# Inverse square roots: from a seed and three Newton steps on VectorE to one power instruction on GpSimd

## The chip, the cores and the metric

The kernel runs on one core of a Trainium2 chip, in one launch. The metric is device microseconds. TensorE (PE) multiplies matrices into PSUM, VectorE (DVE) and ScalarE (ACT) work on tiles in SBUF and PSUM, GpSimd (POOL) works on tiles in SBUF and issues some DMAs, SyncE (SP) issues most DMAs. Each engine takes its instructions in the order of its own program, and waits at an instruction whose operands aren't there.

## The reference

Two blocks of a network on 512 tokens of 1024 channels, in float32: in the first a pooling mixer, attention and two gated feed-forward layers; in the second, twice, a layer that mixes four branches (a sparse attention, a retention, a recurrence of the RWKV kind, a short convolution), then cross attention to a memory of 256 tokens, then a feed-forward layer. Norms stand before and after the parts. Three computations in it need an inverse square root:

```python
def rmsnorm(x, g):
    y = xf * lax.rsqrt(jnp.mean(xf * xf, axis=-1, keepdims=True) + EPS)
def head_norm(u, eps):
    return (u - mu) * lax.rsqrt(var + eps)
```

and the unit length of the keys in the recurrence, per head and token.

## The kernel before

Activations are kept with channels on the 128 partitions: eight tiles of 128 x 512 for 1024 channels. To multiply in float32, weights and activations are split into a high part (hi) and the rest (lo); each 128 x 128 weight chunk is fetched by SP (tile wraw), its high part made by ScalarE (whi, L346) and the rest by VectorE (wlo, L347, 128 x 1024), and three matmuls (L356 to L358) follow for each input tile. A matmul of 512 columns is the common unit on TensorE.

A norm works in steps. As the tiles of x are made, ScalarE squares them (L422), GpSimd adds the squares up (L431, tile sq), and TensorE sums them over the channels with tokens on the partitions (L449, `stat_sum`): one number per token, 128 x 4 for all 512 tokens or 128 x 2 for a half. `stat_end` then takes mean and epsilon on VectorE (L463, tile rstv), calls `rsqrt`, spreads the result over all partitions by four transposes on TensorE (L467) and copies it to SBUF on ScalarE (L468, tile rstd). For a norm before a part, the part's first matmuls are started on the unscaled x ("lead", tiles hhi and hlo), and the factor is applied when their results leave PSUM; the statistic so runs beside matmuls. For a norm after a part (`post`), the normed tiles need the factor: VectorE multiplies (L932, or L929 in the final norm of the first block) and adds to x (L935), then splits into hhi and hlo (L395). In four of these (`post` with fill) products for the memory's keys and values (`mem_kv`, tile vm, L874 and L876) run on TensorE meanwhile. The last norm of the kernel goes by halves of the tokens, with half of the additions on GpSimd, and ends in the output's DMAs.

`head_norm` (eight calls: four in the recurrence, whose result is transposed at L1266, four in the retention, transposed at L1492) takes the variance at L1008 (tile hn, 128 x 8), calls `rsqrt` and multiplies at L1010. The keys' unit length (four calls) is limited at L1076 (tile kn, 128 x 8), goes through `rsqrt`, is spread by a copy (L1079) and transposed (L1082). Macc is the sum of the four branches, which GpSimd adds up at L1536.

`rsqrt` itself (L397 to L408) shifts the number's bits right by one (L402), subtracts them from a constant (L403), halves and negates the number (L404), and takes three Newton steps of three operations each (L406 to L408), all on VectorE, on tiles of 2, 4 or 8 columns; tile rs is its scratch. There are 33 calls: 21 from `stat_end`, 8 from `head_norm`, 4 for keys.

The program is written as one sequence of such calls. A scheduler then orders each engine's instructions by its own estimates of when they will be ready, so an instruction that is shorter, longer or on another engine moves others too.

Of the kernel before, what the change touches and what calls it, by code (L numbers as in the profile page):

```python
# [10 lines left out]
F32 = mybir.dt.float32  # L11
F32R = mybir.dt.float32r
I32 = mybir.dt.int32
AF = mybir.ActivationFunctionType
OP = mybir.AluOpType
AX = mybir.AxisListType

P = 128
# [21 lines left out]
# ---------------------------------------------------------------- host layout  # L40
# [112 lines left out]
def pack(inputs):  # L153
# [24 lines left out]
    # second block  # L178
# [49 lines left out]
# ---------------------------------------------------------------- kernel  # L228
class Two:
    """Eight column tiles kept in two tiles of four."""  # L230
# [8 lines left out]
class Kern:  # L239
    def __init__(self, ctx, tc, a, vat):  # L240
        self.tc, self.nc, self.a, self.vat = tc, tc.nc, a, vat
        pool = lambda name, bufs, **k: ctx.enter_context(tc.tile_pool(name=name, bufs=bufs, **k))
        self.const = pool("const", 1)
        self.big = pool("big", 1)
        self.wp = pool("wp", 3)
        self.wk = pool("wk", 2)
        self.ps = pool("ps", 1, space=bass.MemoryType.PSUM)
        self.turn, self.dtags, self.led, self.held = 0, ("pmm", "pr"), [], []
        self.dram = pool("dram", 2, space=bass.MemoryType.DRAM)
        nc = self.nc  # L250
        self.x = self.bigt("x", F32, "rbig")
        self.cst = self.const.tile([P, _CONST.n], F32, name="cst")
        self.vec = self.const.tile([P, a["vec"].shape[1]], F32, name="vec")
        nv = vat["norm_mix0"][1]
        nc.scalar.dma_start(self.vec[:, :nv], a["vec"][:, :nv])
        one = self.const.tile([P, 1], F32, name="one")
        nc.vector.memset(one, 0.0)
        nc.scalar.activation(one, one, AF.Exp)
        first = self.leads("pool_in")
        raws = self.half("w01", F32).rearrange("p k t -> p (k t)").rearrange("p (c k m) -> p c k m", c=2, k=KD)  # L260
        raws = [raws[:, 0], raws[:, 1], self.wtile("wraw")]
        self.held = [(self.wtile("whi"), self.wtile("wlo")) for _ in range(3)]

        def xload(ks):
            for k in ks:
                nc.sync.dma_start(self.x[:, k], a["xT"][:, k])

        xload([0])
        for part, then in ((slice(0, 4), (1, 2, 3)), (slice(4, 8), (4, 5, 6, 7))):
            for raw, ap, (hi, lo) in zip(raws, first, self.held):  # L270
                nc.sync.dma_start(raw[:, part], ap[:, part])
                nc.scalar.activation(hi[:, part], raw[:, part], AF.Copy)  # L272
                nc.vector.tensor_sub(lo[:, part], raw[:, part], hi[:, part])
            xload(then)
        nc.sync.dma_start(self.cst, a["cst"])
        nc.sync.dma_start(self.vec[:, nv:], a["vec"][:, nv:])
        self.load_phase(_CONST1, a["cst1"])
        self.ident = self.c("ident")
        self.ones = self.c("ones")[:, 0:1]
        self.nsplit = 0  # L280

    # ---- small pieces
# [67 lines left out]
    def products(self, ps, wt, xh, xl, ks, cols, first=True, last=True):  # L350
        """ps[:, cols] (+)= the chunk wt's products with x's tiles ks, in three exact-split passes."""
        nc = self.nc
        hi, lo = wt
        for i, k in ks:
            a, z = first and i == ks[0][0], last and i == ks[-1][0]
            nc.tensor.matmul(ps[:, cols], hi[:, i], xh[:, k, cols], start=a, stop=False)  # L356
            nc.tensor.matmul(ps[:, cols], hi[:, i], xl[:, k, cols], start=False, stop=False)  # L357
            nc.tensor.matmul(ps[:, cols], lo[:, i], xh[:, k, cols], start=False, stop=z)  # L358

    def hold(self, aps):  # L360
        """Fetches the chunks that the next lead starts with."""
        self.held = [self.weights(ap) for ap in aps]

    def dense(self, ap, xh, xl, ks=None, width=T, ps=None, then=()):
        """ps[128 cols, width] = W^T x for the column chunk ap [128, kt, 128]; the chunks then are fetched behind it."""
# [9 lines left out]
    def lead(self, aps, xh, xl, nh, order=range(KD)):  # L375
        """Starts the chunks aps together, following x's tiles as they come; the next calls of dense return them."""
# [20 lines left out]
    def rsqrt(self, out, v, n):  # L397
        """out = v ** -0.5 on [128, n], v positive and normal."""
        nc = self.nc
        s = self.wk.tile([P, 3, 16], F32, name="rs", tag="rs", bufs=2)  # L400
        i, h, t = s[:, 0, :n], s[:, 1, :n], s[:, 2, :n]
        nc.vector.tensor_scalar(i.bitcast(I32), v.bitcast(I32), 1, None, op0=OP.logical_shift_right)  # L402
        nc.vector.tensor_scalar(out.bitcast(I32), i.bitcast(I32), -1.0, float(0x5F3759DF), op0=OP.mult, op1=OP.add)  # L403
        nc.vector.tensor_scalar(h, v, -0.5, None, op0=OP.mult)  # L404
        for _ in range(3):
            nc.vector.tensor_mul(t, out, out)  # L406
            nc.vector.tensor_mul(t, t, h)  # L407
            nc.vector.scalar_tensor_tensor(out, t, 1.5, out, op0=OP.add, op1=OP.mult)  # L408

    # ---- rms norm of a feature-major tile: statistics  # L410
# [5 lines left out]
    def stat_feed(self, st, src, last, half=None, lazy=False):  # L416
        """Adds the squares of src, all of a tile or one half of its tokens, to the statistics."""
# [23 lines left out]
    def stat_sum(self, st, hs):  # L441
        """The sums over the channels, tokens on partitions."""
# [9 lines left out]
    def stat_end(self, st, half=None):  # L452
        """rstd, the same on all partitions, of the tokens of one half or of both."""
# [20 lines left out]
    # ---- pre-norm: x * g split, statistics running along  # L474
# [19 lines left out]
    # ================================================================ first block  # L494
    def leads(self, what, i=0):
        """The chunks that a part starts with."""
# [39 lines left out]
    def proj_add(self, w, hi, lo, nxt, then):  # L536
        """x += w^T (hi + lo), feeding the next norm."""
# [7 lines left out]
    def ffn(self, i, pn, nxt_name):  # L545
        """With nxt_name, feeds the next norm; without, ends in the final norm and feeds the second block's first."""
# [49 lines left out]
    def rope(self, pa, pb, c, s, dst, j):  # L596
        """Rotates halves pa/pb (4 heads) into dst[:, j:j+2], two heads to a tile, halves interleaved."""
# [15 lines left out]
    def pipelined(items, first, second, depth=1):  # L613
        """second(item) comes depth items after first(item)."""
# [10 lines left out]
    def cls(ap, g, b):  # L625
        """Columns (tokens) of block b of group g, of a [.., T] access pattern."""
# [5 lines left out]
    def natural(ap, g):  # L632
        """[.., (block, position)] viewed in token order."""
# [5 lines left out]
    def tok(ap, g):  # L639
        """[.., T] split to match natural()."""  # L640
# [4 lines left out]
    def attention(self, pn, nxt):  # L645
# [30 lines left out]
        # scores, softmax, values  # L676
# [47 lines left out]
        for g in range(3):  # L724
            hs = slice(H0[g], H0[g] + HG[g])
            st = self.wk.tile([P, 4, 2], F32, name=f"st{g}", bufs=1)
            # group statistics: -max and sum over heads of den * exp(m - max)
# [67 lines left out]
    # ================================================================ second block  # L795
    def bias_tables(self):
        """Relative bias by distance, queries on partitions: [:, h, c] for distance q - c + 384."""
# [47 lines left out]
    def mem_kv(self, i, count, hl, psums):  # L845
        """The next count chunks of the memory's keys [P, 8, 256], feature-major, and values [P, 2, 1024], to DRAM.

        hl is a place for the split memory. Returns what emits the products, which hang on nothing else."""
# [54 lines left out]
    def post(self, w, xh, xl, y, add, gname, nxt, then=(), out=None, fill=None):  # L903
        """y (+)= W^T x over the column chunks w, then x += rmsnorm(y) * g (x = rmsnorm(x) * g where y is x).

        The last chunks go by halves of the tokens, so that the norm of one half runs beside the other's products."""
# [14 lines left out]
        def norm(group):  # L921
            """The normed tiles of the (tile, columns, half) in group, one stage behind another."""
# [52 lines left out]
    # ---- mixers  # L975
# [13 lines left out]
    def sigmoid(self, out, src, bias=0.0):  # L989
        """sigmoid(src + 2 * bias) through tanh."""  # L990
# [3 lines left out]
    def head_norm(self, alloc, y, nseg, eps):  # L994
        """(y - mean) * rstd over the last 64 of PSUM y [P, nseg, 64], to SBUF."""
# [17 lines left out]
    def rwkv_in(self, l):  # L1013
        """Token-shifted projections: r, k, v (two tiles each) and the low-rank inputs."""
# [20 lines left out]
    def rwkv(self, l, j, out):  # L1035
        """Heads 2j and 2j + 1, in chunks of 64 tokens; out [P, T] feature-major."""
# [12 lines left out]
        # decay  # L1049
# [14 lines left out]
        # a, gate  # L1064
# [4 lines left out]
        # normalised k  # L1069
# [19 lines left out]
        # scaled operands  # L1089
# [12 lines left out]
        # bonus: sum over channels of r k r_k, times v  # L1102
# [6 lines left out]
        # token-major copies  # L1109
# [11 lines left out]
        # products within a chunk  # L1121
# [11 lines left out]
        # inverse of I - A: blocks of 16 by substitution, then doubled twice  # L1133
# [78 lines left out]
        # the chunks in order  # L1212
# [61 lines left out]
    def nsa(self, l, W, out, cw):  # L1274
# [9 lines left out]
        # selected and window keys and values  # L1284
# [5 lines left out]
        # gates, token-major: [P, 4, 12]  # L1290
# [28 lines left out]
        # compressed keys and values  # L1319
# [109 lines left out]
    def retention_in(self, l, W, vN):  # L1429
        """Rotated q, k in W[:, 0:4], token-major v in the two tiles vN."""  # L1430
# [17 lines left out]
    def retention_gate(self, on, hi, lo):  # L1448
        """Splits silu(g) * on."""
# [9 lines left out]
    def retention(self, l, W, vN):  # L1459
        """Normalised heads times half the gain, feature-major, in place of vN."""  # L1460
# [55 lines left out]
    def merge(self, m, hi, lo, acc, out=None, ns=range(KD)):  # L1516
        """acc (+)= 2 sigmoid(gate m) * branch m; the last one splits half of the sum into out."""
# [195 lines left out]
```

## Time and profile before

| | |
|---|---|
| median of 3 runs | 3460.29 us (3453.46 to 3465.56) |
| span of the profiled execution, first to last instruction | 3453.0 us, the only time of its own that it has |
| mean granted TensorE clock | 0.983 |
| TensorE (PE) busy | 97% |
| VectorE (DVE) busy | 53% |
| ScalarE (ACT) busy | 34% |
| GpSimd (POOL) busy | 11% |

The span lies 7.3 us under the median of the runs and inside their range. In a timeline the first two columns are the start and the duration in us, then engine, line and operation, the tiles written and read, their shapes, the count of instructions merged into the row, and in brackets the idle time before it and what ended it. A matmul of 512 columns is shown with 0.39 us, but matmuls overlap: the next one starts 0.22 to 0.23 us after it.

### The profile page before, as it was taken

Reading aid. Unit: us, or ns where it says so; the run is one execution under the profiler, and the core shown is the slowest. Engines: PE = TensorE matmul, PEld = TensorE weight load, DVE = VectorE, ACT = ScalarE, POOL = GpSimd, SP = SyncE. Lnnn points to the kernel's source line nnn. Section 1 sums busy time; section 2 is a strip of 40 time slices with the busy share of each in tenths; the row PEclk is TensorE's granted clock in tenths of the full one; section 3 lists DMA queues with packets and bytes.
Section 4 is the critical chain, followed back from the end, with each engine's and each line's share of the span. In section 5 each row is a group of like instructions: output and inputs, shape, how many; then the busy total and the mean of one; then the engine's idle time right before and its main releaser. Section 6 shows DMA issues by size and latency. Waiting matters only on the chain. (4 is left out here: it accounts for less than half of the span.)

```text
span 3453.0 us, 41910 instructions
## 1 busy us (share of the span) xinstructions
PE 3358.4 (97%) x16382; PEld 2685.1 (78%) x16382; DVE 1829.7 (53%) x3340; ACT 1168.0 (34%) x1947; POOL 391.5 (11%) x328
## 2 busy tenths in 40 slices
PE   8999999999999999999999999998999999999997
PEld 6888888787888777777887788886777788688886
DVE  7554444445544465656455544556565644664445
ACT  4332232443322323322244433342332234343332
POOL 3200012001000120101220200012010122120001
PEclk9999999989999999999999999999999999999998
DMA  3323235223222330232242333333123223223332
GB/s 131 104 98 96 93 103 155 77 86 115 95 97 94 102 105 32 72 106 87 93 145 68 104 98 98 98 110 115 34 56 96 88 92 124 84 68 98 98 98 67
DMA packets 105718, 326.29 MB, mean 94 GB/s; under 512 B 13288, under 2 KB 16880, under 8 KB 103472
## 3 DMA queue, kind: packets, MB, share of 16 engines
q1 hardware_dynamic: 99600, 295.68, 26.3%
q10 hardware_dynamic: 3232, 19.28, 1.5%
q0 software_dynamic: 2688, 8.66, 1.2%
q8 instruction: 128, 2.10, 0.3%
q14 instruction: 70, 0.57, 0.1%
HBM read 305.47 MB, written 11.81 MB: 92 GB/s over the span
## 5 line engine op out<-in xcount | busy, mean ns | idle before, releaser
L346 ACT ACTIVATE whi<-wraw 128x1024 fp32r<-128x1024 f32 (+3 forms) x593 | 565.0, 954 | 1605.8 <-PE pmm L357 638.9
L347 DVE TENSOR_TENSOR wlo<-wraw,whi 128x1024 fp32r<-128x1024 f32 (+3 forms) x593 | 654.3, 1104 | 217.4 <-ACT whi L346 212.5
L357 PE MATMUL pmm<-hlo,whi 128*128 128x512 f32 (+1 forms) x1504 | 599.2, 398 | 13.1 <-DVE hlo L395 12.8
L358 PE MATMUL pmm<-hhi,wlo 128*128 128x512 f32 (+1 forms) x1504 | 597.7, 397 | 1.7 <-DVE wlo L347 1.7
L356 PE MATMUL pmm<-hhi,whi 128*128 128x512 f32 (+1 forms) x1504 | 597.5, 397 | 0.0
L357 PE MATMUL pr<-hlo,whi 128*128 128x512 f32 (+1 forms) x1048 | 411.2, 392 | 10.2 <-DVE hlo L395 9.8
L356 PE MATMUL pr<-hhi,whi 128*128 128x512 f32 (+1 forms) x1048 | 409.8, 391 | 9.3 <-ACT whi L272 6.4
L358 PE MATMUL pr<-hhi,wlo 128*128 128x512 f32 (+1 forms) x1048 | 409.1, 391 | 0.8 <-DVE wlo L347 0.8
L431 POOL TENSOR_TENSOR sq<-sq 128x512 f32<-128x512 f32 (+1 forms) x130 | 181.2, 1394 | 1784.3 <-ACT sq L422 1754.2
L357 PEld LDWEIGHTS pmm<-hlo,whi 128*128 128x128 f32 x1504 | 285.9, 190 | 83.5 <-DVE hlo L395 18.4
L358 PEld LDWEIGHTS pmm<-hhi,wlo 128*128 128x128 f32 x1504 | 286.1, 190 | 64.4 <-DVE wlo L347 4.6
L356 PEld LDWEIGHTS pmm<-hhi,whi 128*128 128x128 f32 x1504 | 285.5, 190 | 58.8 <-issue 1.0
L357 PEld LDWEIGHTS pr<-hlo,whi 128*128 128x128 f32 x1048 | 199.6, 190 | 55.4 <-DVE hlo L395 15.5
L356 PEld LDWEIGHTS pr<-hhi,whi 128*128 128x128 f32 x1048 | 199.5, 190 | 51.1 <-ACT whi L272 6.3
L358 PEld LDWEIGHTS pr<-hhi,wlo 128*128 128x128 f32 x1048 | 199.4, 190 | 44.1 <-DVE wlo L347 4.0
L1536 POOL TENSOR_TENSOR macc<-macc,g 128x512 f32<-128x512 f32 x48 | 69.6, 1452 | 347.9 <-DVE g L1535 240.0
L358 PE MATMUL pmm<-ahi,wlo 128*128 128x512 f32 x240 | 93.4, 389 | 0.0
L356 PE MATMUL pr<-ahi,whi 128*128 128x512 f32 x240 | 93.4, 389 | 0.0
L357 PE MATMUL pr<-alo,whi 128*128 128x512 f32 x240 | 93.4, 389 | 0.0
L358 PE MATMUL pr<-ahi,wlo 128*128 128x512 f32 x240 | 93.4, 389 | 0.0
L356 PE MATMUL pmm<-ahi,whi 128*128 128x512 f32 x240 | 93.4, 389 | 0.0
L357 PE MATMUL pmm<-alo,whi 128*128 128x512 f32 x240 | 93.4, 389 | 0.0
(517 smaller groups left out, 5413.5 us busy)
## 6 DMA issues: line engine op xcount, KB each, us to landing
wraw<-w_in SPq DMA_DIRECT2D x116, 512.0 KB, 3.3
wraw<-mlp SPq DMA_DIRECT2D x64, 512.0 KB, 3.2
wraw<-mlp SPq DMA_DIRECT2D x128, 256.0 KB, 2.8
wraw<-ffn_g SPq DMA_DIRECT2D x44, 512.0 KB, 3.2
wraw<-ffn_u SPq DMA_DIRECT2D x44, 512.0 KB, 3.2
wraw<-wkv SPq DMA_DIRECT2D x32, 512.0 KB, 3.3
wraw<-ffn_d SPq DMA_DIRECT2D x32, 448.0 KB, 3.4
wraw<-qkv SPq DMA_DIRECT2D x24, 512.0 KB, 3.5
```

Of the source, the lines that this page charges most:

```text
L346: nc.scalar.activation(hi[:, :kt, :m], raw[:, :kt, :m], AF.Copy)
L347: nc.vector.tensor_sub(lo[:, :kt, :m], raw[:, :kt, :m], hi[:, :kt, :m])
L356: nc.tensor.matmul(ps[:, cols], hi[:, i], xh[:, k, cols], start=a, stop=False)
L357: nc.tensor.matmul(ps[:, cols], hi[:, i], xl[:, k, cols], start=False, stop=False)
L358: nc.tensor.matmul(ps[:, cols], lo[:, i], xh[:, k, cols], start=False, stop=z)
L431: nc.gpsimd.tensor_add(sq[:, c], acc[h][:, c], sq[:, c])
L1536: nc.gpsimd.tensor_add(acc[:, n], acc[:, n], g)
```

## The change

`rsqrt` becomes one instruction on GpSimd that raises the tile to the power -0.5, with a tile of eight columns of -0.5 that is filled once at the start. Comments and docstrings go too, so line numbers shift by 2 ahead of `rsqrt` and by 6 behind it.

```diff
         nc.scalar.activation(one, one, AF.Exp)
+        self.neghalf = self.const.tile([P, 8], F32, name="neghalf")
+        nc.vector.memset(self.neghalf, -0.5)
...
     def rsqrt(self, out, v, n):
         nc = self.nc
-        s = self.wk.tile([P, 3, 16], F32, name="rs", tag="rs", bufs=2)
-        i, h, t = s[:, 0, :n], s[:, 1, :n], s[:, 2, :n]
-        nc.vector.tensor_scalar(i.bitcast(I32), v.bitcast(I32), 1, None, op0=OP.logical_shift_right)
-        nc.vector.tensor_scalar(out.bitcast(I32), i.bitcast(I32), -1.0, float(0x5F3759DF), op0=OP.mult, op1=OP.add)
-        nc.vector.tensor_scalar(h, v, -0.5, None, op0=OP.mult)
-        for _ in range(3):
-            nc.vector.tensor_mul(t, out, out)
-            nc.vector.tensor_mul(t, t, h)
-            nc.vector.scalar_tensor_tensor(out, t, 1.5, out, op0=OP.add, op1=OP.mult)
+        nc.gpsimd.tensor_tensor(out, v, self.neghalf[:, :n], op=OP.pow)
```

VectorE has 396 instructions fewer and one memset more, GpSimd 33 more. The scheduler moves rows on all engines. VectorE at the norm before the first cross attention (its first results leave PSUM at L1583, after the change L1577), before:

```order
L347 TENSOR_TENSOR wlo<-wraw,whi 128x1024 x2
L463 TENSOR_SCALAR rstv<-pax 128x4
L347 TENSOR_TENSOR wlo<-wraw,whi 128x1024
L402 TENSOR_SCALAR rs<-rstv 128x4
L404 TENSOR_SCALAR rs<-rstv 128x4
L403 TENSOR_SCALAR rstv<-rs 128x4
L406 TENSOR_TENSOR rs<-rstv 128x4
L407 TENSOR_TENSOR rs<-rs 128x4
L408 SCALAR_TENSOR_TENSOR rstv<-rs,rstv 128x4
```

and after, where L457 is the old L463 and L349 the old L347:

```order
L397 SCALAR_TENSOR_TENSOR hlo<-x,vec,hhi 128x512 x3
L349 TENSOR_TENSOR wlo<-wraw,whi 128x1024 x2
L457 TENSOR_SCALAR rstv<-pax 128x4
L349 TENSOR_TENSOR wlo<-wraw,whi 128x1024
L1577 SCALAR_TENSOR_TENSOR xq<-pmm,rstd 128x512
```

L406 to L408 come twice more in the first before L1583 follows; in the second a weight split still stands right behind the statistic. TensorE at the same norm before, from the sums (L449) on; 17 matmuls stand between them and the transposes, of which the last six are shown:

```order
L356 MATMUL pr<-hhi,whi 128x512
L357 MATMUL pr<-hlo,whi 128x512
L358 MATMUL pr<-hhi,wlo 128x512
L356 MATMUL pr<-hhi,whi 128x512
L357 MATMUL pr<-hlo,whi 128x512
L467 MATMUL pax<-cst,rstv 128x128 x4
```

and after, where L443 are the sums and L461 the transposes:

```order
L443 MATMUL pax<-cst,sq 128x1 x4
L358 MATMUL pr<-hhi,whi 128x512
L359 MATMUL pr<-hlo,whi 128x512
L360 MATMUL pr<-hhi,wlo 128x512
L358 MATMUL pr<-hhi,whi 128x512
L359 MATMUL pr<-hlo,whi 128x512
L461 MATMUL pax<-cst,rstv 128x128 x4
```

Twelve matmuls have moved from ahead of the transposes to behind them. Elsewhere the counts between the last sum or product and the transposes go, before to after: 17 to 5 at four norms, 21 to 4 and 24 to 2 at two more, 30 to 4 at three of the four norms with fill products and 33 to 7 at the fourth, 17 to 4 and 20 to 6 at the keys, 44 to 28 and 64 to 42 at the recurrence's head norms, 34, 35, 34 and 33 to 19, 22, 19 and 19 at the retention's; in the stretch of halves 51 to 13, 73 to 4 and 19 to 4; at two norms 60 stay, at three none.

GpSimd at the end of the first layer's recurrence, before (L1269 adds the recurrence's bonus, L1536 the branches):

```order
L602 TENSOR_TENSOR ra<-ra,rt 128x512
L606 TENSOR_TENSOR rb<-rb,rt 128x512
L1536 TENSOR_TENSOR macc<-macc,g 128x512 x2
L1269 TENSOR_TENSOR yt<-yt,rz 128x512
L1536 TENSOR_TENSOR macc<-macc,g 128x512 x6
```

and after (L402 is the power, L1263 and L1530 the two additions):

```order
L596 TENSOR_TENSOR ra<-ra,rt 128x512
L600 TENSOR_TENSOR rb<-rb,rt 128x512
L402 TENSOR_TENSOR hn<-hn,neghalf 128x8
L1263 TENSOR_TENSOR yt<-yt,rz 128x512
L1530 TENSOR_TENSOR macc<-macc,g 128x512 x4
L402 TENSOR_TENSOR hn<-hn,neghalf 128x8 x2
L1530 TENSOR_TENSOR macc<-macc,g 128x512 x4
```

The recurrence's last power and the addition that hangs on it have moved ahead of the branches' additions; the retention's two powers stand between those.

## Rows read from the trace of the kernel before

**Rows 1.** The page's first part: busy us, share of the span, instructions

```profile
PE 3358.4 (97%) x16382; PEld 2685.1 (78%) x16382; DVE 1829.7 (53%) x3340; ACT 1168.0 (34%) x1947; POOL 391.5 (11%) x328
```

**Rows 2.** Waits: engine, line, what ended them, us, times, longest

```profile
PE pax L467 <- DVE rstv L408: 12.5, 5, 6.6
```

**Rows 3.** Tile rs: operation, count, ns shortest/median/longest, first and last start

```profile
L407 DVE TENSOR_TENSOR rs<-rs x99: 148/163/1283, 31.8 to 3437.8; 128x4 f32<-128x4 f32 x42, 128x8 f32<-128x8 f32 x36, 128x2 f32<-128x2 f32 x21
```

**Rows 4.** Timelines of two uncovered statistics: start us, duration, engine, line, [idle before]

```profile
1193.88 0.16 DVE L463 TENSOR_SCALAR rstv<-pax 128x4 f32<-128x4 f32 x1 [1.09 <-PE pax L449]
...
1196.37 1.09 PE L467 MATMUL pax<-cst,rstv 128*128 128x128 f32 x4 [2.52 <-DVE rstv L408]
...
2346.93 0.65 PE L467 MATMUL pax<-cst,rstv 128*128 128x128 f32 x4 [2.43 <-DVE rstv L408]
```

**Rows 5.** Timeline of one covered statistic (DVE, then PE)

```profile
1829.04 0.16 DVE L463 TENSOR_SCALAR rstv<-pax 128x4 f32<-128x4 f32 x1
1829.12 1.22 DVE L347 TENSOR_TENSOR wlo<-wraw,whi 128x1024 fp32r<-128x1024 f32 x1
...
1832.62 0.39 PE L357 MATMUL pr<-hlo,whi 128*128 128x512 f32 x1
1832.84 0.60 PE L467 MATMUL pax<-cst,rstv 128*128 128x128 f32 x4
```

**Rows 6.** Timeline of one normalised k (DVE, then PE)

```profile
1252.87 0.17 DVE L1076 TENSOR_SCALAR kn<-pr 128x8 f32<-128x8 f32 x1 [1.19 <-PE pr L1074]
...
1256.30 0.43 DVE L1079 COPY kb<-kn 128x512 f32<-128x512 f32 x1
...
1256.78 0.66 PE L1082 MATMUL pr<-cst,kb 128*128 128x128 f32 x4
```

**Rows 7.** Who waited for tile hn (us, times)

```profile
  PE pr L1266: 2.4, 2
```

**Rows 8.** Stretches: length, PE, PEld, DVE, ACT, POOL busy, PEclk, DMA share, GB/s

```profile
1796.70:1818.00 21.30, 16.83 (x84) 13.10 (x82) 21.30 (x26) 11.29 (x17) 11.39 (x8) 0.92 0.58 209
...
3056.00:3100.00 44.00, 39.56 (x258) 35.70 (x258) 39.86 (x106) 21.23 (x48) 14.13 (x16) 0.92 0.19 62
...
35.00:80.00 45.00, 37.19 (x153) 28.93 (x151) 42.55 (x87) 16.52 (x29) 16.45 (x12) 0.92 0.17 56
```

**Rows 9.** Timeline of VectorE at one statistic with fill products behind it

```profile
1791.68 0.16 DVE L463 TENSOR_SCALAR rstv<-pax 128x4 f32<-128x4 f32 x1 [1.53 <-PE pax L449]
...
1793.82 1.22 DVE L347 TENSOR_TENSOR wlo<-wraw,whi 128x1024 fp32r<-128x1024 f32 x1
...
1795.15 0.16 DVE L408 SCALAR_TENSOR_TENSOR rstv<-rs,rstv 128x4 f32<-128x4 f32 x1
1796.36 0.42 DVE L874 TENSOR_TENSOR vm<-pr,mr 128x256 f32<-128x256 f32 x1 [1.05 <-PE pr L358]
1796.71 1.41 DVE L932 SCALAR_TENSOR_TENSOR pt<-yb,vec,rstd 128x512 f32<-128x512 f32 x2
```

**Rows 10.** Timeline of the last statistic (DVE, then PE)

```profile
3432.23 0.16 DVE L463 TENSOR_SCALAR rstv<-pax 128x2 f32<-128x2 f32 x1 [0.64 <-PE pax L449]
...
3438.53 0.16 DVE L408 SCALAR_TENSOR_TENSOR rstv<-rs,rstv 128x2 f32<-128x2 f32 x1
...
3438.84 0.66 PE L467 MATMUL pax<-cst,rstv 128*128 128x128 f32 x2 [6.64 <-DVE rstv L408]
```

**Rows 11.** GpSimd: two undisturbed adds, one beside a split, descriptor writing by form

```profile
1552.53 1.29 POOL L1536 TENSOR_TENSOR macc<-macc,g 128x512 f32<-128x512 f32 x1 [29.55 <-DVE hn L1008]
...
3429.63 0.73 POOL L431 TENSOR_TENSOR sq<-sq 128x256 f32<-128x256 f32 x1 [1.39 <-ACT sq L422]
...
114.48 0.75 DVE L395 SCALAR_TENSOR_TENSOR hlo<-x,vec,hhi 128x512 fp32r<-128x512 f32 x1
...
114.58 1.80 POOL L431 TENSOR_TENSOR sq<-sq 128x512 f32<-128x512 f32 x1 [3.64 <-issue]
...
L876 POOL DMA_DIRECT2D kd<-vm x16 | 8.9, 556 | 142.2 <-DVE vm L874 123.1 <-DVE rs L407 15.3 <-DVE astat L718 3.8
```

## The prediction

> **What bounds the kernel now.** I read the busy shares first: TensorE is busy in 97% of the span, VectorE in 53%, GpSimd in 11% [rows 1]. So VectorE time that goes is worth nothing unless TensorE or the end waits for it. Next the waits: only five times does TensorE stand still because the last Newton step (L408) releases the transposes (L467), 12.5 us in all [rows 2]. Then the tile rs: a Newton operation takes 163 ns in the median, and L407 alone runs 99 times, three in each of 33 calls [rows 3]; that is 33 x 12 = 396 instructions, some 65 us of VectorE, nearly all of it beside matmuls. The timelines say where the calls matter. They fall into kinds: statistics with nothing behind them on TensorE (1193.88 and 2346.93) [rows 4]; statistics with a lead of matmuls behind them [rows 5]; the four key norms [rows 6]; the eight head norms, two of which end in a wait of TensorE [rows 7]; four statistics followed by a stretch that VectorE fills without a gap (21.30 of 21.30 us), and two more stretches that it nearly fills [rows 8, 9]; and the last statistic, where Newton is mixed with other norm work [rows 10].
>
> **The price that no row shows.** The trace has no power instruction. Call X2, X4 and X8 the time of one on 2, 4 and 8 columns. Undisturbed adds take 1.29 us for 512 columns and 0.73 for 256 [rows 11], so 2.2 ns a column and 0.17 us beside. The lower end is then about 0.2 us for any of the three widths, a power as cheap as an add. The upper end is as long as the twelve operations it replaces, 2.1 us for 4 columns (the 2.33 us between L463's end and the transposes in [rows 4], less hand-overs), so 0.48 us a column. The nearest row is the 0.556 us of the engine's descriptor writing [rows 11], work that it also does step by step; I take X4 = 0.6, so 0.11 us a column beside the 0.17: X2 = 0.40, X4 = 0.62, X8 = 1.06. Hand-overs: L408's end to the transposes is 0.15 us (3438.69 to 3438.84) [rows 10]; for the new step from VectorE to GpSimd I take 0.1, an estimate of the same size.
>
> [...]
>
> **The change part by part.** Gains are positive, in us.
> 1. The two uncovered statistics. From L463's end (1194.04) to the transposes (1196.37) 2.33 us pass [rows 4]; afterwards 0.1 + X4 + 0.15. Gain 2.1 - X4 each: 4.2 - 2 X4.
> 2. The end. L463 ends at 3432.39, the transposes start at 3438.84: 6.45 us, since norm operations of the first half and GpSimd adds stand between the Newton steps [rows 10]. Afterwards only the power does, behind an add of GpSimd that may be running (0.8 at most [rows 11]): 1.05 + X2, a gain of 5.4 - X2. The first half's transposes are moved up to four 256-column matmuls behind the sums, which cover 0.5 us, against 0.41 + X2: a stall of X2 - 0.1. The 0.9 us of the two small waits of [rows 2] (12.5 less 6.64, 2.52 and 2.43) goes. Together 6.4 - 2 X2.
> 3. The four statistics with fill products. From L463's end (1791.84) to the first norm operation (1796.71) are 4.87 us, in which VectorE also does a split (1.22) and two evictions (0.42 each) [rows 9]: 2.81 us of no use. Afterwards 0.1 + X4 + the 1.40 from L408's end to the norm, less one eviction: 1.08 + X4. The stretch behind is bound by VectorE [rows 8], so the gain of 1.73 - X4 is kept: 6.9 - 4 X4.
> 4. The pool mixer (35 to 80 us): VectorE 42.55 of 45.00 us, TensorE 37.19 [rows 8]. The statistic ahead of it comes earlier by 2.1 - X4.
> 5. The stretch in halves (3056 to 3100): TensorE idles 4.4 us beside a VectorE busy for 39.86 of 44.00 [rows 8]. Four calls go, 7.8 us of VectorE. I take 3 us, less 2 X2, since its last two transposes now stand four matmuls behind their sums.
> 6. Four statistics whose lead covered them. The order takes 12 matmuls out from between sums and transposes (17 before, 5 after; at one 21 before, 4 after). At 0.22 us each [rows 5] the turn of the transposes moves from 1832.84 to about 1830.2. On VectorE a weight split (1829.12, 1.22 us) starts right behind L463. An add that started 0.1 us after a 0.75 us split took 1.80 us, not 1.29 [rows 11]: it was held 0.51 of the 0.65 left. The power, due at 1829.3, so starts at about 1830.2 and reaches TensorE at 1830.35 + X4. Stall 0.2 + X4 each: -0.8 - 4 X4.
> 7. One more such pair at 141 us: -0.8.
> 8. Four key norms. L1076 ends at 1253.04, then 0.1 + X8 + 0.1 + the copy's 0.43 + 0.1; the transposes' turn moves 13 matmuls up, from 1256.78 to 1253.8 [rows 6]. Stall X8 - 0.15 each: +0.6 - 4 X8.
> 9. Eight head norms. Two waits, 2.4 us, go [rows 7]; there the order still leaves 42 rows between product and transposes. At the other six it takes out 13 to 16 rows, some 3.3 us, as much as undisturbed Newton and one split (2.1 + 1.2) took: stall X8 less 0.13. Together 3.2 - 6 X8.
>
> At 493 and 834 us sixty matmuls stay between sums and transposes: nothing. The sum: 24.8 - 11 X4 - 10 X8 - 4 X2 = 24.8 - 6.8 - 10.6 - 1.6 = 5.8 us. In c, the us per column: 20.5 - 132 c. A gain of 6 off the span of 3453.0 is 3447; the median of the runs stands 7.3 above that span, so 3454.3.
>
> [...]
>
> **Rivals.** (a) The power is nearly as cheap as an add (c = 0.03): X4 = 0.3, all covers hold, and 20.5 - 4 = 16.5 us go: 3444. For it: GpSimd is 89% idle and the operands are tiny. Against it: no elementwise function of the trace is a power. It begins at c = 0.077. (b) The transposes and key and head norms that were moved up stall TensorE: the place is L467, L1082, L1266 and L1492 in their new rows, the price X4 or X8 for each of 4, 4 and 6 sites, and it turns the sign at c = 0.155 and passes 0.3% at c = 0.234 (X4 = 1.1). At c = 0.33 it is 23 us slower, 3483; at the upper end 43, 3503. For it: TensorE had no wait at these sites before, so all of it is new. Against: it needs a power more than twice as long as descriptor writing. (c) VectorE's relief is worth more than points 3 to 5, as its stretches are longer than I count: some 5 us more, which leads into (a).
>
> **How the numbers follow.** Differences below 0.3% (10.4 us) can't be told from none here. Between c = 0.077 and 0.234 the result is within that: 0.37, my forecast, with a range of its own from 3450 to 3471. Faster, (a) with (c): 0.34. Slower, (b): 0.29. The range goes from the lower end of the price (X = 0.2: 24.8 - 5.0 = 19.8, 3441) to short of its upper end, 3496, with 0.06 left out below and 0.13 above.
>
> **What would show it.** The powers' own durations on GpSimd first: 0.6 us on 4 columns, 1.1 on 8. New waits of TensorE for GpSimd at the transposes (0.8 us at the four leads, 0.9 at keys and heads), the waits of 2.5 and 2.4 us down to 0.9, the last one from 6.6 to about 1.5, and the last statistic some 5 us nearer the end. The stretch behind each fill statistic should begin about 1 us earlier. If the powers last over 1.1 us on 4 columns, or TensorE waits at the old covers for longer than a matmul or two, (b) holds; if these waits are missing, (a) does.

## The result, and the profile after

| | before | after |
|---|---|---|
| median of the runs shown together | 3462.93 us (4 runs, 3453.46 to 3468.34) | 3498.73 us (4 runs, 3496.46 to 3504.75) |
| ratio of the times, 95% interval | | 1.0105 [1.0086, 1.0125] |
| profiled execution: span, its own time | 3453.0 | 3497.9, 3499.72 |
| mean granted TensorE clock there | 0.983 | 0.976 |

Slower by 36 us, where no change was forecast; the time lies 2.7 us above the upper end of the range. The busy shares of the page after (engine, us, share, instructions) answer to [rows 1]:

```profile
PE 3387.8 (97%) x16382; PEld 2705.4 (77%) x16382; DVE 1773.9 (51%) x2945; ACT 1168.1 (33%) x1947; POOL 440.0 (13%) x361
```

VectorE lost 56 us of work and TensorE was busy 29 us longer with the same 16382 matmuls; its idle time (span less busy) grew from 94.6 to 110.1 us. The power's own durations (count: ns shortest/median/longest, first and last start) are the number that no row of before had:

```profile
L402 POOL TENSOR_TENSOR rstv<-rstv,neghalf x21: 708/1024/1960, 28.8 to 3482.8; 128x4 f32<-128x4 f32 x14, 128x2 f32<-128x2 f32 x7
L402 POOL TENSOR_TENSOR hn<-hn,neghalf x8: 1637/2113/2583, 1399.4 to 2781.3; 128x8 f32<-128x8 f32 x8
L402 POOL TENSOR_TENSOR kn<-kn,neghalf x4: 1640/1644/1650, 1251.8 to 2569.9; 128x8 f32<-128x8 f32 x4
```

Undisturbed it takes 0.71 us on 2 columns, 1.02 on 4 and 1.64 on 8. These lie on a line of 0.155 us a column with 0.40 beside; I had taken 0.40, 0.62 and 1.06. The waits of TensorE (what waits, what released it: us, times, longest), to be read against [rows 2, 7]:

```profile
PE pax L461 <- POOL rstv L402: 15.1, 16, 1.4
PE pmm L360 <- DVE wlo L349: 7.0, 8, 3.0
PE pmm L358 <- ACT whi L348: 6.6, 7, 1.1
PE pr L1076 <- DVE kb L1073: 4.9, 4, 1.4
PE pr L1260 <- DVE hc L1004: 4.2, 4, 1.3
PE pax L1486 <- DVE hc L1004: 3.4, 3, 1.4
```

The transposes behind a power now wait at 16 statistics, at all keys and at seven of eight head norms. The rows for whi and wlo have nothing to do with a power: there the products of weight chunks wait for the chunk's split. Three timelines after: an uncovered statistic and the covered one of [rows 4, 5], and the last one [rows 10]:

```profile
1192.07 0.16 DVE L457 TENSOR_SCALAR rstv<-pax 128x4 f32<-128x4 f32 x1 [1.09 <-PE pax L443]
1192.31 1.02 POOL L402 TENSOR_TENSOR rstv<-rstv,neghalf 128x4 f32<-128x4 f32 x1 [4.93 <-DVE rstv L457]
...
1193.39 1.11 PE L461 MATMUL pax<-cst,rstv 128*128 128x128 f32 x4 [1.36 <-POOL rstv L402]
...
1849.33 1.23 DVE L349 TENSOR_TENSOR wlo<-wraw,whi 128x1024 fp32r<-128x1024 f32 x1
1849.49 1.96 POOL L402 TENSOR_TENSOR rstv<-rstv,neghalf 128x4 f32<-128x4 f32 x1 [5.88 <-DVE rstv L457]
...
1851.51 0.65 PE L461 MATMUL pax<-cst,rstv 128*128 128x128 f32 x4 [1.03 <-POOL rstv L402]
...
3482.51 0.16 DVE L457 TENSOR_SCALAR rstv<-pax 128x2 f32<-128x2 f32 x1 [0.50 <-PE pax L443]
...
3483.72 0.69 PE L461 MATMUL pax<-cst,rstv 128*128 128x128 f32 x2 [1.24 <-POOL rstv L402]
```

The uncovered wait falls from 2.52 to 1.36 us, the last from 6.64 to 1.24. At the covered one the power lasts 1.96 us instead of 1.02, and a VectorE split runs beside it. I measured both traces from statistic to statistic. The stretch from the first keys to the statistic behind the mixers (1253 to 1792 before, and again 2382 to 2922) grows by 21 and 20 us, 41 of the span's 45. In each of the two stands a piece of 20.48 us at half clock that the trace of before does not have, behind the wait at L1486; the first is shown (the second view: length, PE, PEld, DVE, ACT, POOL busy, PEclk, DMA share, GB/s):

```profile
1600.30 0.66 PE L1486 MATMUL pax<-cst,hc 128*128 128x128 f32 x4 [1.44 <-DVE hc L1004]
```

```profile
1580.00:1602.10 22.10, 20.66 (x99) 14.36 (x98) 11.26 (x21) 4.21 (x5) 2.93 (x2) 1.00 0.14 49
1602.10:1622.60 20.50, 20.50 (x63) 14.95 (x62) 7.25 (x13) 1.16 (x2) 0.00 (x0) 0.50 0.23 78
```

TensorE gets 63 matmuls done in 20.5 us there, against 99 in the 22.1 us just ahead of it. Over the whole span the trace shows 167 us at half clock after, 121 before. So three suspects: the power's price at the transposes, the new order (the waits for weights), and the clock.

### The profile page after: what moved, and what is told of

Read it like the earlier page. It is cut to its first block, busy times and chain, and to the rows that moved or that the text cites. A ratio compares the mean times of both kernels' runs of the same rounds, so it can differ in the third digit from the quotient of the medians.

```text
span 3497.9 us, 41559 instructions
## 1 busy us (share of the span) xinstructions
PE 3387.8 (97%) x16382; PEld 2705.4 (77%) x16382; DVE 1773.9 (51%) x2945; ACT 1168.1 (33%) x1947; POOL 440.0 (13%) x361
## 5 line engine op out<-in xcount | busy, mean ns | idle before, releaser
L349 DVE TENSOR_TENSOR wlo<-wraw,whi 128x1024 fp32r<-128x1024 f32 (+3 forms) x593 | 655.5, 1106 | 230.1 <-ACT whi L348 225.2
L360 PE MATMUL pmm<-hhi,wlo 128*128 128x512 f32 (+1 forms) x1504 | 601.1, 400 | 6.5 <-DVE wlo L349 6.4
L358 PE MATMUL pmm<-hhi,whi 128*128 128x512 f32 (+1 forms) x1504 | 599.3, 399 | 6.6 <-ACT whi L348 6.6
L358 PE MATMUL pr<-hhi,whi 128*128 128x512 f32 (+1 forms) x1048 | 412.6, 394 | 10.4 <-ACT whi L274 6.2
L360 PE MATMUL pr<-hhi,wlo 128*128 128x512 f32 (+1 forms) x1048 | 411.4, 393 | 2.0 <-DVE wlo L349 2.0
L360 PEld LDWEIGHTS pmm<-hhi,wlo 128*128 128x128 f32 x1504 | 287.0, 191 | 72.6 <-DVE wlo L349 11.3
L358 PEld LDWEIGHTS pmm<-hhi,whi 128*128 128x128 f32 x1504 | 286.7, 191 | 68.0 <-ACT whi L348 9.8
L358 PEld LDWEIGHTS pr<-hhi,whi 128*128 128x128 f32 x1048 | 200.7, 192 | 53.1 <-ACT whi L274 6.2
L360 PEld LDWEIGHTS pr<-hhi,wlo 128*128 128x128 f32 x1048 | 200.4, 191 | 46.1 <-DVE wlo L349 5.5
L1530 POOL TENSOR_TENSOR macc<-macc,g 128x512 f32<-128x512 f32 x48 | 69.7, 1452 | 256.7 <-DVE g L1529 252.4
L360 PE MATMUL pmm<-ahi,wlo 128*128 128x512 f32 x240 | 93.4, 389 | 0.0
L358 PE MATMUL pr<-ahi,whi 128*128 128x512 f32 x240 | 93.4, 389 | 0.0
L360 PE MATMUL pr<-ahi,wlo 128*128 128x512 f32 x240 | 93.4, 389 | 0.0
L358 PE MATMUL pmm<-ahi,whi 128*128 128x512 f32 x240 | 93.4, 389 | 0.0
```

The costliest lines, as they stand in the source:

```text
L349: nc.vector.tensor_sub(lo[:, :kt, :m], raw[:, :kt, :m], hi[:, :kt, :m])
L1530: nc.gpsimd.tensor_add(acc[:, n], acc[:, n], g)
```

## The experiments

Each was timed against runs of the kernel before on the same chip. Each run also lists its mean granted clock. Over the 57 runs of before in these comparisons it goes from 0.976 to 0.985 and the time from 3472 down to 3450: 2.34 us less for 0.001 more (a straight line through them). Kernels can so be compared at one clock; the last column moves every run to 0.980 along the slope within all kernels, 2.40 us. With the clock listed to 0.001, such a value is good to about 1 us where there are six runs or fewer.

| | power where | median us | ratio to before [95%] | mean clock | us at 0.980 |
|---|---|---|---|---|---|
| before | nowhere | | 1 | 0.9804 | 3462.2 |
| after | all 33 | 3498.73 | 1.0105 [1.0086, 1.0125] | 0.9765 | 3491.3 |
| e1_stat | 21 statistics | 3461.25 | 1.0003 [0.9984, 1.0021] | 0.9811 | 3464.5 |
| e2_head | 8 head norms | 3484.46 | 1.0074 [1.0048, 1.0100] | 0.9795 | 3485.7 |
| e3_keys | 4 keys | 3478.58 | 1.0052 [1.0035, 1.0070] | 0.9793 | 3476.8 |
| e4_cheap | all, as multiplications | 3453.95 | 0.9975 [0.9960, 0.9989] | 0.9848 | 3465.9 |
| e5_ret | all, retention's 4 as multiplications | 3487.35 | 1.0079 [1.0058, 1.0101] | 0.9798 | 3486.5 |
| e6_rec | all, recurrence's 4 as multiplications | 3490.82 | 1.0092 [1.0068, 1.0116] | 0.9788 | 3486.2 |
| e7_post | 9 statistics behind parts | 3450.39 | 0.9968 [0.9952, 0.9983] | 0.9830 | 3456.5 |
| e8_keys_cheap | 4 keys, as multiplications | 3480.25 | 1.0056 [1.0040, 1.0072] | 0.9785 | 3476.7 |
| e9_head_cheap | 8 head norms, as multiplications | 3465.98 | 1.0020 [1.0010, 1.0030] | 0.9823 | 3472.7 |

**One kind of call at a time.** Newton stays in the others.

```diff
-        self.rsqrt(v[:, 1, t0:t1], v[:, 0, t0:t1], t1 - t0)
+        self.rsqrt(v[:, 1, t0:t1], v[:, 0, t0:t1], t1 - t0, True)        # e1_stat: the power
...
-        self.rsqrt(sm[:, 3, :nseg], sm[:, 2, :nseg], nseg)
+        self.rsqrt(sm[:, 3, :nseg], sm[:, 2, :nseg], nseg, True)         # e2_head
...
-        self.rsqrt(kn[:, 1], kn[:, 0], 8)
+        self.rsqrt(kn[:, 1], kn[:, 0], 8, True)                          # e3_keys
```

> The power only in the 21 norm statistics; Newton stays in the head norms and the keys. Theory A (the loss is made in the recurrence and retention stretches, where the changed kernel's trace grows by about 19.5 us in each layer): no loss here, between 5 us faster and 5 us slower than before (ratio 0.9985 to 1.0015), and no half-clock stretch at the retentions. Theory B (every transpose that was moved up stalls by the power's time, everywhere alike): my sum with the measured 0.71 and 1.02 us gives 7 us faster for these calls (0.998). Theory C (any change of order costs, wherever it is): 10 us or more slower.

> The power only in the eight head norms. Theory A: most of the loss, 30 to 40 us slower than before (ratio 1.009 to 1.012), with new waits of TensorE at L1266 and L1492 and a half-clock stretch of about 20 us in each layer's retention. Theory B: 3.2 - 6 x 1.64 = 7 us slower (1.002). Theory C: some 10 us slower.

> The power only for the four keys. Theory A: up to 6 us slower (ratio 1.000 to 1.002). Theory B: 0.6 - 4 x 1.64 = 6 us slower (1.0017). Theory C: 10 us or more slower. If the keys, and not the head norms, throw the recurrence's schedule about, the 30 to 40 us show here.

The statistics cost nothing (1.0003): theory A holds there, theory C falls, and the 7 us of gain that B gave don't come. Head norms cost 26 us, a little less than A said, and the keys 18, three times what A or B allowed. The parts add up to 1.29%, more than the whole's 1.05% (at one clock 40 us against 29), so heads and keys seem to share a loss.

**The price alone.** The changed kernel with another operation in the same place. Every engine has the same instructions in the same order as after.

```diff
-        nc.vector.memset(self.neghalf, -0.5)
+        nc.vector.memset(self.neghalf, 1e-5)
...
-        nc.gpsimd.tensor_tensor(out, v, self.neghalf[:, :n], op=OP.pow)
+        nc.gpsimd.tensor_tensor(out, v, self.neghalf[:, :n], op=OP.mult)
```

> The changed kernel with its 33 powers turned into GpSimd multiplications by a constant of the same tiles, in the same order on every engine; so the inverse square roots are left out and only the price of the operation differs. Theory P (the power's duration is the loss): the multiplications take some 0.2 to 0.4 us, the stalls at the transposes and the half-clock stretches of 20 us in the retentions go, and the time is that of my sum with X = 0.3, about 15 us faster than before (ratio 0.9955). Theory O (the new order, or the way over GpSimd, is the loss): it stays 25 us or more slower than before (1.007 and up), with the half-clock stretches.

The shortest multiplications take 0.20 us, as do the medians at statistics and keys; some last up to 1.15 us, and what lengthened those isn't shown:

```profile
L402 POOL TENSOR_TENSOR rstv<-rstv,neghalf x21: 196/203/1145, 30.8 to 3435.6; 128x4 f32<-128x4 f32 x14, 128x2 f32<-128x2 f32 x7
L402 POOL TENSOR_TENSOR hn<-hn,neghalf x8: 202/658/1118, 1396.3 to 2740.6; 128x8 f32<-128x8 f32 x8
L402 POOL TENSOR_TENSOR kn<-kn,neghalf x4: 206/208/208, 1248.7 to 2542.0; 128x8 f32<-128x8 f32 x4
```

At one order, then, the price of the power moves the time by 45 us (0.9975 against 1.0105): 25.4 at one clock, the rest is the clock (0.9848 against 0.9765). My sum's coefficients for the difference of the prices, 11 x 0.82 + 10 x 1.43 + 4 x 0.51, give 25.4 too (by kind they fit less well, see below). Theory P is right in sign, and short: the sum with these prices promised 24.8 - 5.1 = 20 us less than before, and 9 came. The rest stays as a loss that a cheap operation doesn't lift, and the profile says where: from the statistic ahead of the mixers to the one behind them e4 takes 6.9 us longer than before in the first layer and 8.6 in the second (579.0 and 586.3 us against 572.1 and 577.8), and 18 us less in all the rest. Half clock is only part of that: 7 us more of it in those two stretches, 28 us less in the rest. The stalls at the transposes are nearly gone (3.9 us for L461, none at keys and head norms), while the waits for the weights' high parts are there as after:

```profile
PE pmm L358 <- ACT whi L348: 6.8, 8, 1.1
```

**The order alone.** The same replacement in e3_keys and e2_head, again with unchanged orders.

```diff
-        nc.vector.memset(self.neghalf, -0.5)
+        nc.vector.memset(self.neghalf, 1e-5)
...
-        if pw: return self.nc.gpsimd.tensor_tensor(out, v, self.neghalf[:, :n], op=OP.pow)
+        if pw: return self.nc.gpsimd.tensor_tensor(out, v, self.neghalf[:, :n], op=OP.mult)
```

> The kernel with the power only at the keys, in its own order, with those four powers turned into multiplications of the same tiles (the keys' inverse square roots are left out). Theory O (half of the keys' loss of 18 us is the new order: w_in chunks that wait 0.92 and 0.52 us for their weights three times in each layer, 8.7 us): the price of four powers goes, 4 x 1.43 = 6 us, and some 9 to 12 us stay: ratio to before 1.0025 to 1.0035, with the waits for whi in the trace. Theory P (the whole loss is the power's time and what follows from it): 0.9985 to 1.0005.

> The kernel with the power only in the head norms, in its own order, with those eight powers turned into multiplications of the same tiles (the head norms' inverse square roots are left out). Theory O: 8 x 1.43 = 11 us go and some 12 to 15 us stay, 8.7 of them the waits for whi and wlo that this kernel's trace shows too: ratio to before 1.0035 to 1.0045. Theory P: 0.9985 to 1.0005.

The keys' loss is all order: 1.0056 with multiplications of 0.20 us, 1.0052 with powers of 1.66. Theory P falls there, and O erred in granting the price 6 us. At the heads 1.0020 lies between the two theories' ranges: 19 of 26 us are price and 7 order (13 and 10.5 at one clock). What the order does shows at 1448 to 1471 in the trace after. The products of a gate's chunk (pmm, L358 to L360) wait for its own split, and the split has waited for the matmul that frees its buffer:

```profile
1454.31 1.06 ACT L348 ACTIVATE whi<-wraw 128x1024 fp32r<-128x1024 f32 x1 [4.78 <-PE pmm L359]
1461.78 1.06 ACT L348 ACTIVATE whi<-wraw 128x1024 fp32r<-128x1024 f32 x1 [5.88 <-PE pmm L359]
1476.59 1.06 ACT L348 ACTIVATE whi<-wraw 128x1024 fp32r<-128x1024 f32 x1 [4.86 <-PE pax L1524]
...
1455.42 0.50 PE L358 MATMUL pmm<-hhi,whi 128*128 128x512 f32 x1 [0.92 <-ACT whi L348]
1456.68 0.50 PE L360 MATMUL pmm<-hhi,wlo 128*128 128x512 f32 x1 [0.52 <-DVE wlo L349]
...
1471.06 0.47 PE L1523 MATMUL pax<-mixhl,whi 128*128 128x512 f32 x1
```

Before, a branch chunk's products (mixhl) went mostly six at a time between the gates' chunks, and no chunk waited:

```profile
1469.45 1.06 ACT L346 ACTIVATE whi<-wraw 128x1024 fp32r<-128x1024 f32 x1 [4.81 <-issue]
...
1469.43 0.39 PE L1529 MATMUL pax<-mixhl,whi 128*128 128x512 f32 x1
...
1470.79 0.39 PE L356 MATMUL pmm<-hhi,whi 128*128 128x512 f32 x1
```

The split of 1469.45 ends at 1470.51 and its low part takes 1.22 us more, too late for the chunk that starts at 1470.79; so it is the next one's, a whole chunk ahead. After, three gates run through first and 36 branch products follow in one block from 1471.06. Each split starts as the chunk before lets go of its buffer, and the next chunk starts as the split ends. So of the three weight buffers (WHL = 3) one turns over here. The other two hold the branch's chunks: the split of 1476.59 waits for a branch product (L1524) that frees a buffer, 24 products into the block, and the last twelve follow without a pause, from a chunk that was split earlier. Each layer has three waits of 0.92 us and two of 0.52, 7.6 us for both. e8_keys_cheap, whose operation costs next to nothing, has three pairs a layer, 2 x 3 x 1.45 = 8.7 us:

```profile
1463.22 0.50 PE L356 MATMUL pmm<-hhi,whi 128*128 128x512 f32 x1 [0.97 <-ACT whi L346]
1464.48 0.50 PE L358 MATMUL pmm<-hhi,wlo 128*128 128x512 f32 x1 [0.53 <-DVE wlo L347]
1472.29 0.50 PE L356 MATMUL pmm<-hhi,whi 128*128 128x512 f32 x1 [0.92 <-ACT whi L346]
```

The row pmm <- whi sums to 5.5 or 5.6 us in e2, e3, e8 and e9, 1.1 in e1 and nothing before: these waits are what head norms and keys share. No run has a fourth buffer, which would test them directly. They aren't all loss, for other waits get shorter. The pages' first lines for e9 (span 3463.4) and e8 (3479.9):

```profile
PE 3361.9 (97%) x16382; PEld 2686.7 (78%) x16382; DVE 1812.0 (52%) x3245; ACT 1166.5 (34%) x1947; POOL 389.7 (11%) x336
PE 3380.0 (97%) x16382; PEld 2697.4 (78%) x16382; DVE 1817.1 (52%) x3293; ACT 1169.4 (34%) x1947; POOL 393.8 (11%) x332
```

In e9, which has as much half clock as before (120 us), TensorE idles 6.9 us more and is busy 3.5 us more: that is the 10.4 us by which its span is longer. In e8 it idles 5.3 us more and is busy 21.6 us more. How much of that busy time is the order's own isn't pinned down: e8's trace shows 35 us more at half clock than before, one 20.5 us stretch of it at the recurrence (same columns as above):

```profile
2554.30:2574.80 20.50, 20.50 (x62) 14.59 (x61) 10.15 (x22) 7.81 (x15) 0.20 (x1) 0.50 0.00 0
```

**The half-clock stretches of the retention.** The order of after, with four of its powers made multiplications.

```diff
-        nc.gpsimd.tensor_tensor(out, v, self.neghalf[:, :n], op=OP.pow)
+        nc.gpsimd.tensor_tensor(out, v, self.neghalf[:, :n], op=op)
...
-        self.rsqrt(sm[:, 3, :nseg], sm[:, 2, :nseg], nseg)
+        self.rsqrt(sm[:, 3, :nseg], sm[:, 2, :nseg], nseg, OP.mult if alloc == self.w2k else OP.pow)   # e5_ret; e6_rec: self.rt
```

> The changed kernel in its own order, with only the retention's four powers turned into multiplications of the same tiles (those four inverse square roots are left out). Theory S (each power costs only the stall at its own transposes): the waits at L1486 (1.44, 0, 1.43 and 0.57 us) go, some 3 to 4 us less than the changed kernel, so about 3495 (ratio to before 1.009). Theory H (the stall there is also what the clock falls after, and each layer's half-clock stretch of 20.48 us, worth some 10 us, goes with it): some 24 us less, about 3474 (1.003).

> The changed kernel in its own order, with only the recurrence's four head powers turned into multiplications (those four inverse square roots are left out). Theory S: the waits at L1260 (0.78, 1.32, 0.77 and 1.29 us) go, some 4 us less than the changed kernel, about 3494 (ratio to before 1.009). Theory H, that the half-clock stretches follow the stall at L1486 behind the second retention power and not the recurrence's: the same 4 us, the two stretches of 20.48 us stay. If they go here, the stall at L1486 isn't what they follow, and the time is about 3474.

They take 4.8 and 5.1 us away at one clock, about one more than their stalls of 3.4 and 4.2 (theory S). By the ratios it is 9 and 4 us, and the intervals overlap that of after. The two stretches of 20.48 us are gone from e5's profile, as theory H said, but from e6's too, where TensorE still waits 1.45 us at the same place and the clock stays full:

```profile
1592.76 0.66 PE L1486 MATMUL pax<-cst,hc 128*128 128x128 f32 x4 [1.45 <-DVE hc L1004]
```

```profile
1585.00:1610.00 25.00, 22.94 (x120) 17.31 (x120) 12.66 (x25) 3.71 (x5) 3.31 (x2) 1.00 0.19 64
```

So that wait stands with and without half clock behind it, and H isn't shown. Runs of e6 alone have mean clocks from 0.975 to 0.984 and times from 3501 to 3477. What can be said is the mean: the changed kernel's runs lie at 0.9765, before's at 0.9804, worth some 9 us. The same order with multiplications everywhere (e4_cheap) runs at 0.9848, so in that order the lower clock comes with the powers; at the keys alone it is 0.9793 with powers and 0.9785 without. What brings it stays open.

**Only where nothing covers.** The power in the statistics of `post` alone.

```diff
-            self.stat_end(st)
+            self.stat_end(st, None, True)
...
-                self.stat_end(st, 0)
+                self.stat_end(st, 0, True)
...
-        self.stat_end(st, 1)
+        self.stat_end(st, 1, True)
```

> Newton everywhere but in the statistics of the norms behind a part, where nothing or little covers the wait (the two uncovered ones, the four with fill products, the two stretches by halves with the last norm); no pre-norm, no key and no head norm. By the terms of my sum with the measured 0.71 and 1.02 us: 4.2 - 2.0 at the uncovered ones, 6.4 - 1.4 at the end, 6.9 - 4.1 at the fills, 3 - 1.4 in the halves: some 11 us faster than before (ratio 0.997). Rival, from the power in all statistics (1.0003): what the fills and halves gain is given back behind them, and only the end's 4 to 5 us are left (0.9985 to 0.999).

0.9968 [0.9952, 0.9983], 11 us faster than before: the sum's value, and a lower time than that of before or after. One of the two uncovered statistics turned out to be a pre-norm and kept Newton. At one clock the gain is 5.7 us, near the rival's; the rest goes with a clock of 0.9830, so that the full 11 us agree with the sum is partly luck. The last norm gives 4 us of it: from its statistic on 15.4 us instead of 20.8, less 1.3 lost ahead of it.

## Why the prediction was wrong

Forecast 6 us of gain, measured 36 of loss: 42 us, which come in three parts.

1. **The price of the power was mis-sized: 11 us.** X4 = 0.62 was taken near the 0.556 us of the descriptor writing [rows 11]; that the two kinds of work are alike was my estimate, which no run shows. It is 1.02, and 0.71 and 1.64 on 2 and 8 columns. With these the sum is 24.8 - 11.2 - 16.4 - 2.8 = -5.6 us. That is rival (b)'s direction: the slope is its turning point of 0.155 us a column, and the 0.40 beside goes past it. But 5.6 us are still inside the 10.4 that the prediction called no change, so the price alone doesn't make the forecast wrong. Taken together the coefficients fit (25.4 by the sum and by the runs), one by one they don't: for the keys they give 4 x 1.43 = 5.7 us and e3 against e8 shows 0.1, for the heads 6 x 1.43 = 8.6 (8 x 1.43 = 11.4, had the two waits that stayed been counted) and e2 against e9 shows 13. So the agreement of the total is partly luck. The bounds held: a multiplication takes 0.20 us, the lower end, and the power on 4 columns half of the upper.
2. **The constant of 24.8 was too large by some 23 us: the step that failed.** At one clock e4_cheap should have been 20 us below before, and is 3.7 above. In points 8 and 9 I counted the matmuls between a product and its transposes, and took the other moved rows for free. They were not: moving the keys alone brings an order that costs 14.5 us at one clock, the heads alone one that costs 10.5, with some 9 us of new waits for weight buffers in either. Those lie at products that no power touches, so no counting at the transposes finds them. The kernels e8 and e9 have orders of their own, so the two losses aren't shares of the 23; in the order of after the weight waits are 7.6 us, and what makes up the rest there isn't shown. Its place is shown: the two stretches of the mixers, where e4's profile is 15.5 us longer. The prediction showed the order of GpSimd at that place, but not that of TensorE's weight chunks. The statistics give less than points 1 to 7 as well: with the measured prices 7 us of gain, measured 2.3 of loss at one clock.
3. **The clock: some 9 us.** The runs of after have a mean clock of 0.9765, those of before 0.9804, and the sum has no term for the clock. In e4_cheap, the same order without the powers' price, it is 0.9848; so this part hangs on the price too, but by what way isn't shown.

By points, with the measured X: most stalls came where they were said to. Point 1: gain 1.08 each, measured 1.16 and 1.06 (2.52 to 1.36, 2.43 to 1.37). Point 2: 5.0, measured 4.0. Point 3: 0.7 at each of four fills, measured 0.2 in the mean from one statistic to the next (0.7 in e7's trace). Point 5: 1.6 in the halves, measured 0.3. Point 6: 1.22 each, measured 1.03 to 1.24. The longer time beside a split that it counts came too: the power of 1849.49 took 0.94 us more than an undisturbed one, with 1.07 us of the split still to run. Point 7: 0.8, measured 0.46; its term leaves out the price of the two powers there. Point 8: 1.49, measured 1.42, 1.02, 1.42 and 1.02; by its own terms (1253.77 + X8 against 1253.8) the stall is X8 less 0.03, not 0.15, half a us in the sum. Point 9: at six places 1.5, measured 0.6 to 1.4 at five and none at one. The two waits of 2.4 us in all [rows 7] were to go, and stayed, at 1.32 and 1.29 us: the power there stands beside a split and lasts 2.58 us, so the 42 rows left between product and transposes don't cover it. In e4_cheap there is no wait at this place.

```profile
1546.56 2.58 POOL L402 TENSOR_TENSOR hn<-hn,neghalf 128x8 f32<-128x8 f32 x1 [3.17 <-DVE hn L1002]
...
1550.02 0.63 PE L1260 MATMUL pr<-cst,hc 128*128 128x128 f32 x4 [1.32 <-DVE hc L1004]
```

Rival (a) fell by the power's durations. Nothing shows (c): the halves and the fills, where VectorE's relief was to count, gained less than points 3 and 5 say.

## What to carry to other kernels

Before, TensorE waited at the transposes behind eight of the 33 Newton calls only (five at L467, two at L1266, one of 0.3 us at L1492, 15.2 us in all). At the other 25 there was no wait of TensorE to win, and moving them to another engine moved much that the scheduler places by them (the keys' order alone cost 14.5 us at one clock, with an operation of 0.20 us): compare the order of the weight chunks and of their buffers, not only the rows around the moved instruction. Here a power on GpSimd (1.02 us for twelve VectorE operations of 2.1) paid behind the parts, where little covers the wait (e7_post, 0.9968), not where most of Newton ran beside matmuls (1.0074 at the head norms, 1.0052 at the keys). To split a loss into price and order, put an operation of another price at the same place in the same order.

## What was not expected of the hardware

The power's time grows by 0.155 us for each column from 2 to 8 (0.71, 1.02 and 1.64 us), while the multiplication's stays at 0.20 us. Nearly the whole spread between the runs of before follows the mean granted clock: 57 runs lie within 23 us, and 0.009 of clock accounts for 21 of them. Behind waits of the same length a stretch falls to half clock at one place and not at another: in e2_head's profile one of 23.9 us in the first layer's retention and none in the second's, where TensorE waited as long (1.4 us).
